# Unmasked retention products, sample states read in fours, mixer-output loads placed earlier, and gate steps moved into two stages of a hybrid decoder layer

## The chip, the cores and the metric

The kernel runs on one core of a Trainium2 chip. The metric is the device time of one execution in microseconds (us). TensorE (PE) multiplies, with its weight loads listed apart as PEld; VectorE (DVE), ScalarE (ACT) and GpSimd (POOL) work on tiles in the on-chip memory; SyncE (SP) issues most DMAs, in order, and POOL issues the gathers of cache pages. A "row" of PE is one record of the profile. A product of two plain fp32 tiles leaves two PE rows; one of fp32r tiles, and a transpose, leaves one.

## The reference, cut to what matters

One layer for 1024 prompt tokens and 64 sample tokens (8 sequences of 8 tokens), model width 1024: feed-forward, mixer, feed-forward. The mixer projects the normed input `u` once (`w_in`) and has two branches, each behind gates:

```python
# stick-breaking attention: 8 heads x 64, strictly causal; the sample tokens also see 2048 cached positions
# retention: 4 heads, key width 128, value width 256, over chunks
inner = einsum('bhcd,bhsd->bhcs', qi, ki) * decay_in      # zero where s > c
o = einsum('bhcs,bhsv->bhcv', inner, vi) + einsum('bhcd,bhdv->bhcv', qi, S) * decay_q
S = S * decay_c + einsum('bhsd,bhsv->bhdv', ki * decay_k, vi)
...
m = sigmoid(a_sb) * (o_sb @ w_sb_out) + sigmoid(a_r) * (o_r @ w_ret_out);  h = h + RMSNorm_post(m @ w_o)
```

Each sample sequence brings its own retention state of 128 x 256 per head, which is read by its 8 queries and returned updated. `decay_in` is zero above the diagonal.

## The kernel before, in words

All activations lie transposed (features on the 128 partitions, tokens along the free dimension). A product of full precision is `mm3` (L132 to L138): both factors are split into a high and a low fp32r part, and three fp32r matmuls (high weights times high data, L133; high weights times low data, L137; low weights times high data, L138) add up in one bank of PSUM. There are eight banks: two named `pa`, two `pb`, three `pc`, one `pm`.

The order of the run: the first feed-forward (0 to about 790 us), `mixer_in` (to about 1925 us), `mixer_out` (to about 2065 us), the second feed-forward, and the last norm.

`mixer_in` runs these parts:

- Retention, heads r = 0 to 3 (`retention`, L1305). A head projects queries, keys and values (`dense`), computes two gates, prepares the sample tokens, and goes over four chunks of 256 prompt tokens. A chunk transposes its keys (L1437), forms scores for two key halves s = 0, 1 against all 256 queries (`pz`), multiplies by the decay mask `rdec` (512 columns, zero above the diagonal), splits the result, multiplies it by the values (`po`), adds the state's part, normalises (`finish`) and updates the state. For s = 1 the first 128 queries lie wholly above the diagonal.
- After each chunk `sample_states` (L1388) takes two of the eight sample sequences. It loads their states into `s0` (two buffers), multiplies each with that sequence's queries, laid out as 64 columns of which 8 are not zero (L1394, fp32, 64-column weights), forms the outer products of keys and values (L1399, fp32, 128-column weights), and stores the new states from the same tile.
- The prompt's attention, heads 0 to 7 (`prompt_sb`, L889), with each pair's projections, and then the sample tokens' attention over the cache (`decode_sb`). Its pages come by 128 gathers of 512 KB (`kp`, `vp`), and its small products run four side by side, each on 32 columns of the array (`side_by_side`, L1129).

Beside these runs a list of independent tiles of work, the gates and the projection by `w_ret_out` (`gate_steps`, `ret_steps`). One step is one `mm3`; eight steps make one bank's result, which goes through a tile `gs` (three buffers) to DRAM. `fill(k)` takes k steps from the list. Before the change 40 steps are taken after the last retention head (`FILL_RET`, behind the head's last transposes), 2 at each of the 16 places of prompt heads 0, 2, 4, 6 and 7, 12 after the prompt (`FILL_SB`), and the rest in the decode at 1.6, 1.75 or 2 steps a place, until the list is empty.

The order within each engine's queue is made ahead of time by a planner, which takes the instructions by program order as their inputs come free by its own costs and keeps the hand-written ordering edges (`behind`, `high_priority`). A queue on the chip then runs strictly in that order.

`mixer_out` multiplies the attention output (`attn_parts` loads and splits it; the sample part comes from `osD`) by `w_sb_out` in three token pieces c = 0, 1, 2 of 512, 288 and 288 tokens, eight output tiles d each. Each result is multiplied by a gate tile `g` and added to a tile `m` (both `xr`, eight buffers, L1581 and L1583), and split (`mh`, `ml`). The loads of piece c + 1 are issued at d = 4 of piece c, with their split behind them.

Of the kernel before, what the change touches and what calls it, by code (L numbers as in the profile page):

```python
# [19 lines left out]
P = 128  # L20
# [21 lines left out]
FILL_RET, FILL_SB = 40, 12  # L42
# [26 lines left out]
class Trunk:  # L69
# [700 lines left out]
    def gates_out(self, specs, pool=None, ahead=()):  # L770
# [19 lines left out]

    def gate_steps(self, specs, after=None, chunks=(0, 1, 2)):
# [4 lines left out]
        for c in chunks:  # L796
            o, n = CH[c]
            for (wh, wl), (_, row, _) in zip(ws, specs):
                ps = self.bank("pa")
                for k in range(KD):  # L800
                    self.mm3(ps[:, :n], wh[:, k, :], wl[:, k, :], self.u[0][c][:, k, :n], self.u[1][c][:, k, :n],
                             k == 0, k == KD - 1)
                    if k == KD - 1:
                        g = self.t(self.gstage, [P, 384], "gs", bufs=3)
                        nc.scalar.activation(g[:, :n], ps[:, :n], AF.Sigmoid)
                        nc.sync.dma_start(row[:, o : o + n], g[:, :n])
# [52 lines left out]
    def ret_steps(self, d):  # L859
# [4 lines left out]
        for c, (o, n) in enumerate(CH):  # L864
# [3 lines left out]
            for k in range(KD):  # L868
                self.mm3(ps[:, :n], wh[:, k, :], wl[:, k, :], self.ro[0][c][:, k, :n], self.ro[1][c][:, k, :n],
                         k == 0, k == KD - 1)  # L870
                if k == KD - 1:
                    g = self.t(self.gstage, [P, 384], "gs", bufs=3)
# [5 lines left out]
    def through(self, gen, k, other=None):  # L878

        due = 0.0  # L880
        for _ in gen:
            due += k
# [6 lines left out]
    def prompt_sb(self):  # L889
        nc, io = self.nc, self.io  # L890
        win = io["w_in"][0]
        with ExitStack() as ctx:
# [95 lines left out]
            def head(h):  # L988
# [4 lines left out]
                for c in range(4):  # L993
# [29 lines left out]
                    for half in range(2):  # L1023
# [3 lines left out]
                        for g in range(i // 4, -1, -1):  # L1027
                            a = 512 * g
                            w = min(512, n - a)
                            wide = max(w, 256)  # L1030
                            ps = self.bank("pb")
                            lq = qs[:, i * P : (i + 1) * P]
                            nc.tensor.matmul(ps[:, :wide], lq, kh[:, a : a + wide], start=True, stop=False)
                            nc.tensor.matmul(ps[:, :wide], lq, kl[:, a : a + wide], start=False, stop=True)
# [28 lines left out]
            for p in range(4):  # L1063
                self.through(head(2 * p), FILL_HEADS[p][0])
                other = proj(p + 1) if p < 3 else None
                self.through(head(2 * p + 1), FILL_HEADS[p][1], other)
# [5 lines left out]
    def decode_sb(self):  # L1072
# [5 lines left out]
        with ExitStack() as ctx:  # L1078
# [169 lines left out]
            def last_block():  # L1248
# [9 lines left out]
                self.attn_parts(sh, sl, 0, 512)  # L1258
# [46 lines left out]
    def retention(self):  # L1305
        nc, io = self.nc, self.io
        win = io["w_in"][0]
        gam = [1.0 - 2.0 ** (-5 - h) for h in range(RH)]
        with ExitStack() as ctx:
# [7 lines left out]
            ddk = self.t(rp, [64, RH, NB], "ddk")  # L1317
            nc.sync.dma_start(ddk, io["c_ddk"])
            for r in range(RH):
                rdec = self.t(rp, [P, 512], "rdec")  # L1320
# [3 lines left out]
                rq = self.t(rp, [P, RC + TD], "rq")  # L1324
# [5 lines left out]
                vdn = self.t(rp, [P, 256], "vdn")  # L1330
                nc.gpsimd.memset(vdn[64:128, :], 0.0)

                def finish(src, o, n):

                    oc = self.t(rp, [P, 2, RC], "oc", bufs=2)
                    nc.scalar.activation(oc[:, :, :n], src, AF.Copy)
# [24 lines left out]
                def ev_v(vt):  # L1361
                    def ev(c, o, n, ps):
# [12 lines left out]
                        if m < n:  # L1375
                            nc.scalar.activation(vdn[:64, vt * P : (vt + 1) * P], pt[:64, 256:384], AF.Copy)
# [11 lines left out]
                def sample_states(b0):  # L1388
                    s0 = self.t(rp, [P, 2, 256], "s0", bufs=2)
                    nc.sync.dma_start(s0, io["state_ret"][0, b0 : b0 + 2, r].rearrange("b d v -> d b v"))  # L1390
                    pS = self.bank("pm")
                    for j in range(2):
                        b = b0 + j
                        nc.tensor.matmul(po_s[:64, :256], qm[:, b * 64 : (b + 1) * 64], s0[:, j, :],  # L1394
                                         start=False, stop=b == NB - 1)
# [3 lines left out]
                        nc.tensor.matmul(pS[:, j * 256 : (j + 1) * 256], km, vdn, start=True, stop=True)  # L1399
# [6 lines left out]
                sd = self.t(rp, [64, 64], "sd")  # L1406
                nc.vector.tensor_tensor(sd, pz[:64, :64], ddec, op=ALU.mult)
                qm = self.t(rp, [P, 576], "qm")
                nc.gpsimd.memset(qm, 0.0)
                nc.vector.tensor_tensor(qm.rearrange("q (b x) -> q b x", x=72)[:, :, 0:8],  # L1410
                                        qf[:, TP:T].rearrange("q (b t) -> q b t", t=8),
                                        rq[:, RC : RC + TD].rearrange("q (b t) -> q b t", t=8), op=ALU.mult)
                pt = self.bank("pc")
                nc.tensor.transpose(pt[:64, :P], kf[:, TP:T], self.ident)
                kts = self.t(rp, [64, 256], "odn")[:, :P]
                nc.scalar.activation(kts, pt[:64, :P], AF.Copy)
                po_s = self.bank("pc")
                nc.tensor.matmul(po_s[:64, :256], sd, vdn[:64, :], start=True, stop=False)
# [4 lines left out]
                for m in range(TP // RC):  # L1423
# [12 lines left out]
                    for s in range(2):  # L1436
                        nc.tensor.transpose(pt[:, s * P : (s + 1) * P],  # L1437
                                            kf[:, m * RC + s * P : m * RC + (s + 1) * P], self.ident)
# [8 lines left out]
                    sc = self.t(rp, [P, 512], "rsc")  # L1447
                    nc.vector.tensor_tensor(sc, pz, rdec, op=ALU.mult)
                    sch = self.t(rp, [P, 512], "rsch", F32R)
                    scl = self.t(rp, [P, 512], "rscl", F32R)  # L1450
# [10 lines left out]
                    for vt in range(2):  # L1461
                        vc = slice(vt * P, (vt + 1) * P)
                        out = po[:, vt * RC : (vt + 1) * RC]
                        for s in range(2):
                            a = 2 * m + s
                            cc = slice(s * RC, (s + 1) * RC)
                            self.mm3(out, vh[:, a, vc], vl[:, a, vc], sch[:, cc], scl[:, cc],
# [21 lines left out]
                    sample_states(2 * m)  # L1489

                on = self.t(rp, [64, 256], "odn")
                nc.scalar.activation(on, po_s[:64, :256], AF.Copy)
                pt = self.bank("pc")
                for vt in range(2):
                    self.last = nc.tensor.transpose(pt[:, vt * 64 : (vt + 1) * 64], on[:, vt * P : (vt + 1) * P],
                                                    self.ident[:64, :64]).ins
                finish(pt[:, :128].rearrange("q (v c) -> q v c", v=2), TP, TD)
# [39 lines left out]
    def attn_parts(self, sh, sl, o, n):  # L1537

        lf = sl.bitcast(F32)
        m = min(n, TP - o)  # L1540
        for q in range(0, 4, 2):
            qq = slice(q * P, (q + 2) * P)
            self.nc.sync.dma_start(lf[:, q : q + 2, :m], self.osT[qq, o : o + m].rearrange("(k p) t -> p k t", p=P))
            if m < n:
                self.nc.sync.dma_start(lf[:, q : q + 2, m:], self.osD[qq, :].rearrange("(k p) t -> p k t", p=P))
        for q in range(4):
# [3 lines left out]
    def mixer_out(self):  # L1550
        nc, io = self.nc, self.io
        mch = [(0, 512), (512, 288), (800, 288)]
        with ExitStack() as ctx:
# [7 lines left out]
            with ExitStack() as ctx2:  # L1561
# [240 lines left out]
def _constants():  # L1802
# [26 lines left out]
    out["c_rdec"] = rdec.reshape(P, RH, 2 * RC).astype(f)  # L1829
# [3 lines left out]
    out["c_rq"] = np.concatenate([np.exp(lg[:, None] * (c + 1.0)), np.exp(lg[:, None] * (t + 1.0))], 1).astype(f)  # L1833
# [4 lines left out]
    out["c_ddk"] = (np.exp(lg[None, :, None] * (7.0 - t)[:, None, None])  # L1838
                    * (b[:, None] == np.arange(NB)[None, :])[:, None, :] * sc).astype(f)
# [34 lines left out]
```

## Time and profile before

| | |
|---|---|
| times of three runs | 2867.34, 2871.73 (median), 2874.34 us |
| the profiled execution | 2862.49 us; span 2860.0 us, granted clock 0.99 |
| busy: PE, PEld | 2779.8 us (97%), 2638.2 us (92%) |
| busy: DVE, ACT, POOL | 2012.3 us (70%), 1244.4 us (44%), 737.5 us (26%) |
| DMA | 380.63 MB, mean 133 GB/s |

The granted clock is the share of full speed that TensorE was given. Matmuls are pipelined: a matmul's own duration in the profile (some 280 ns for 256 columns) is longer than the time to the next one's start (some 120 ns), so what a matmul costs a busy PE is read from the distance of starts, and "busy" of a group counts overlapped time once per group. A line of the table by stretches gives the stretch and its length, then the busy us (and instructions) of PE, PEld, DVE, ACT and POOL, the granted clock, the DMA engines' share and GB/s. A line of the timeline gives start and duration in us, engine, line, operation, out<-in, the shape and the count; where a merged line holds several shapes, it shows that of the first. In a grouped line stand the count, the group's busy us, the mean ns of one, and the idle time of the engine before them with what ended it.

### The profile page before, as it was taken

The page shows a single profiled execution, that of the slowest core. Times are in us where ns is not written, and L with a number is a line of the kernel's source. Part 1 is how long each engine was busy: PE and PEld are TensorE (multiplying, and loading weights), DVE is VectorE, ACT ScalarE, POOL GpSimd, SP SyncE. Part 2 cuts the span into 40 slices and gives each one's busy share as a digit, 9 for nine tenths or more (in the row PEclk, how much of TensorE's full clock was granted, in tenths as well). Part 3 has the DMA queues.
Part 4 walks back from the last instruction along what each step waited for, and adds up shares of the span by engine and source line. Part 5 has one row for each costly group of instructions (what it writes and reads, how often), then busy time and mean ns, then how long its engine had stood idle before and what let it go on. Part 6 is the DMA issues. An engine that isn't in the chain of part 4 may idle for free.

```text
span 2860.0 us, 51596 instructions
## 1 busy us (share of the span) xinstructions
PE 2779.8 (97%) x20064; PEld 2638.2 (92%) x20064; DVE 2012.3 (70%) x3918; ACT 1244.4 (44%) x2550; POOL 737.5 (26%) x677
## 2 busy tenths in 40 slices
PE   8999999999999999999999999999999999999998
PEld 7898899999989999989999888878989988999997
DVE  7888878888753644544889844445488898688776
ACT  6544444434343333334666642323354444544433
POOL 0234513333150000000001136530113434233331
PEclk9999999999999999999999999999999999999999
DMA  6434444333252323333223379986234346333421
GB/s 186 146 122 146 141 155 125 105 113 111 69 159 88 109 74 92 100 95 102 74 67 88 116 246 334 335 302 190 89 102 132 118 124 197 108 106 102 129 88 38
DMA packets 420868, 380.63 MB, mean 133 GB/s; under 512 B 30800, under 2 KB 381392, under 8 KB 420624
## 3 DMA queue, kind: packets, MB, share of 16 engines
q1 hardware_dynamic: 398352, 306.03, 34.8%
q0 software_dynamic: 22272, 71.31, 7.4%
q8 instruction: 157, 2.57, 0.4%
q14 instruction: 87, 0.71, 0.1%
HBM read 310.03 MB, written 63.05 MB: 130 GB/s over the span
## 4 chain that ended last, share of the span: by engine, by line
PE 61%; DVE 4%; DMA 2%; issue 1%; POOL 1%; ACT 0%; SPq 0%; DVEq 0%; ACTq 0%; POOLq 0%
PE pa L133 10%; PE pa L138 10%; PE pa L137 10%; PE pb L133 4%; PE pb L138 4%; PE pb L137 4%; PE pc L137 3%; PE pc L138 3%; PE pc L133 3%; PE pc L1224 2%; PE pm L1013 1%; PE pm L1129 1%; PE pb L1129 1%; PE pc L1001 1%; DVE sl L99 1%
## 5 line engine op out<-in xcount | busy, mean ns | idle before, releaser
L96 ACT ACTIVATE sh<-wr 128x512 fp32r<-128x512 f32 x592 | 339.3, 622 | 358.4 <-POOL wr L591 136.9
L133 PE MATMUL pa<-uh,wh 128*128 128x384 f32 (+1 forms) x1408 | 471.1, 335 | 4.2 <-ACT qdec L922 2.1
L138 PE MATMUL pa<-uh,wl 128*128 128x384 f32 (+1 forms) x1408 | 465.6, 331 | 0.0
L137 PE MATMUL pa<-ul,wh 128*128 128x384 f32 (+1 forms) x1408 | 464.0, 330 | 0.4 <-POOL ul L99 0.4
L99 DVE TENSOR_TENSOR sl<-wr,sh 128x512 fp32r<-128x512 f32 x592 | 398.2, 699 | 58.5 <-ACT sh L96 55.0
L133 PE MATMUL pa<-q,sh 128*128 128x256 f32 (+1 forms) x1408 | 409.2, 291 | 15.5 <-DVE p L649 7.7
L137 PE MATMUL pa<-q,sh 128*128 128x256 f32 (+1 forms) x1408 | 408.6, 290 | 2.2 <-DVE q L99 2.2
L138 PE MATMUL pa<-q,sl 128*128 128x256 f32 (+1 forms) x1408 | 407.3, 289 | 0.3 <-DVE sl L99 0.3
L137 PE MATMUL pc<-hl,whd 128*128 128x256 f32 (+2 forms) x1088 | 350.4, 324 | 2.6 <-DVE hl L99 2.6
L138 PE MATMUL pc<-hh,wld 128*128 128x256 f32 (+2 forms) x1088 | 349.9, 323 | 0.0
L133 PE MATMUL pc<-hh,whd 128*128 128x256 f32 (+2 forms) x1088 | 343.6, 324 | 4.5 <-DVE y L719 2.5
L719 DVE TENSOR_TENSOR y<-y,pc 128x256 f32<-128x256 f32 (+2 forms) x496 | 249.7, 515 | 134.5 <-PE pc L138 133.0
L133 PE MATMUL pb<-q,sh 128*128 128x288 f32 (+1 forms) x1088 | 314.7, 290 | 6.4 <-ACT sh L96 4.8
L138 PE MATMUL pb<-q,sl 128*128 128x288 f32 (+1 forms) x1088 | 314.4, 289 | 0.5 <-DVE sl L99 0.4
L137 PE MATMUL pb<-q,sh 128*128 128x288 f32 (+1 forms) x1088 | 314.7, 289 | 0.0
L133 PEld LDWEIGHTS pa<-q,sh 128*128 128x128 f32 x1408 | 266.9, 190 | 20.7 <-DVE p L649 8.7
L133 PEld LDWEIGHTS pa<-uh,wh 128*128 128x128 f32 x1408 | 266.5, 189 | 12.3 <-ACT qdec L922 3.2
L137 PEld LDWEIGHTS pa<-q,sh 128*128 128x128 f32 x1408 | 266.7, 189 | 4.9 <-DVE q L99 2.9
L137 PEld LDWEIGHTS pa<-ul,wh 128*128 128x128 f32 x1408 | 266.1, 189 | 2.0 <-POOL ul L99 0.7
L138 PEld LDWEIGHTS pa<-uh,wl 128*128 128x128 f32 x1408 | 265.8, 189 | 2.1 <-issue 1.2
L138 PEld LDWEIGHTS pa<-q,sl 128*128 128x128 f32 x1408 | 265.9, 189 | 1.5 <-DVE sl L99 0.6
L589 POOL TENSOR_TENSOR wr<-wr 128x512 f32<-128x512 f32 x76 | 108.5, 1428 | 497.4 <-DVE sl L99 493.5
(372 smaller groups left out, 5944.6 us busy)
## 6 DMA issues: line engine op xcount, KB each, us to landing
wr<-in_w_ffn_gu_dram SPq DMA_DIRECT2D x176, 512.0 KB
wrd<-in_w_ffn_down_dram SPq DMA_DIRECT2D x88, 512.0 KB
wr<-in_w_in_dram SPq DMA_DIRECT2D x56, 512.0 KB
q<-cB SPq DMA_DIRECT2D x16, 576.0 KB
wr<-in_w_o_dram SPq DMA_DIRECT2D x10, 512.0 KB
cB<-y SPq DMA_DIRECT2D x32, 144.0 KB
cB<-xr SPq DMA_DIRECT2D x32, 144.0 KB
s<-in_state_ret_dram SPq DMA_DIRECT2D x16, 256.0 KB
```

Of the source, the lines that this page charges most:

```text
L96: return self.nc.scalar.activation(dst, src, AF.Copy)
L99: (eng or self.nc.vector).tensor_tensor(dst, src, hi.bitcast(F32), op=ALU.subtract)
L133: ins = mm(ps, wh, xh, start=first, stop=False)
L137: mm(ps, wh, xl, start=False, stop=False)
L138: mm(ps, wl, xh, start=False, stop=last)
L589: tt(v1, v0, v1, op=ALU.add)
L719: nc.vector.tensor_tensor(y[p][:, d, c], y[p][:, d, c], ps[:, :n], op=ALU.add)
L1001: nc.tensor.transpose(tp[:, j * P : (j + 1) * P], bt[:, j * P : (j + 1) * P], self.ident)
L1013: ins = nc.tensor.matmul(po[:, lo:256], vs[:, j, :], ats[j // 4][x][:, j % 4, lo:256], start=(j == 0 and x == 0), stop=(j == last and x == 1))
L1129: return nc.tensor.matmul(out[32 * m : 32 * m + 32], w(m), x(m), start=first, stop=last, skip_group_check=True)
L1224: ins = nc.tensor.transpose(tp[:, i * P : (i + 1) * P], kp[i // 2][:, (i % 2) * 512 + m * P : (i % 2) * 512 + (m + 1) * P], self.ident)
```

## The change

- Unmasked products: scores and values for s = 1 take the last 128 queries only (`seen`); the mask and the split scores have 384 columns. In the prompt attention's scores, blocks of 128 keys are no longer widened to 256 columns.
- Sample states in fours: the queries of a sequence lie in 32 columns (`qs`), and `read_states` multiplies four states side by side, each on 32 columns, at chunks 0 and 2. New states come from fp32r products of `km` and `vxt`, made by a new function `under`, which stacks three high or low copies of a token's values (or keys) under each other by two transposes. `s0` has three buffers, and the first two loads go out before the chunks. The head's own sample scores and the last transposes are laid out accordingly (two products of 128 columns, four transposes).
- Steps of gates: `FILL_RET` goes from 40 to 16; in the last retention head each chunk takes 6 steps behind its own transposes; the last prompt head takes 6 steps instead of 2 at each of its last five places. Tile `gs` has two buffers.
- Mixer output: the loads of piece 1 are issued at d = 0 of piece 0, those of piece 2 at d = 6 of piece 0; the splits stay at d = 4.

```diff
-FILL_RET, FILL_SB = 40, 12
+FILL_CHUNK = 6
+FILL_RET, FILL_SB = 16, 12
+FILL_LAST = 20
...
-                g = self.t(self.gstage, [P, 384], "gs", bufs=3)
+                g = self.t(self.gstage, [P, 384], "gs", bufs=2)
...
-        for _ in gen:
-            due += k
+        for i, _ in enumerate(gen):
+            due += k if more is None else more.get(i, k)
...
-                            wide = max(w, 256)
-                            nc.tensor.matmul(ps[:, :wide], lq, kh[:, a : a + wide], start=True, stop=False)
+                            nc.tensor.matmul(ps[:, :w], lq, kh[:, a : a + w], start=True, stop=False)
...
+                self.through(head(2 * p + 1), FILL_HEADS[p][1], other,
+                             {i: 2 + FILL_LAST / 5 for i in range(11, 16)} if other is None else None)
...
+        seen = slice(0, RC), slice(RC, RC + P)
...
+                def under(src, parts, dst):
+                    xv = ux.rearrange("p (b x) -> p b x", x=32)
+                    sv = src.rearrange("p (b t) -> p b t", t=8)
+                    for i, part in enumerate(parts):
+                        if part == "h":
+                            self.hi(xv[:, :, 8 * i : 8 * i + 8], sv)
+                        else:
+                            self.lo(xv[:, :, 8 * i : 8 * i + 8], sv, xv[:, :, 0:8])
+                    pt = self.bank("pc")
+                    for g in range(2):
+                        nc.tensor.transpose(pt[:, g * P : (g + 1) * P], ux.bitcast(F32)[:, g * P : (g + 1) * P],
+                                            self.ident)
+                    self.hi(dst, pt[:, :256].rearrange("p (g x) -> p g x", x=P))
...
-                        nc.tensor.matmul(po_s[:64, :256], qm[:, b * 64 : (b + 1) * 64], s0[:, j, :],
-                                         start=False, stop=b == NB - 1)
-                        km = self.t(rp, [P, P], "km", bufs=2)
-                        nc.gpsimd.memset(km[64:128, :], 0.0)
-                        nc.vector.tensor_scalar(km[:64, :], kts, ddk[:, r, b : b + 1], None, op0=ALU.mult)
-                        nc.tensor.matmul(pS[:, j * 256 : (j + 1) * 256], km, vdn, start=True, stop=True)
...
+                def read_states(g, s0):
+                    ins = None
+                    for i in (3, 2, 1, 0):
+                        with self.tc.high_priority() if i < 3 else ExitStack():
+                            before, ins = ins, nc.tensor.matmul(
+                                po_s[32 * i : 32 * i + 32, g * 256 : (g + 1) * 256],
+                                qs[:, 32 * (4 * g + i) : 32 * (4 * g + i) + 32], s0[i // 2][:, i % 2, :],
+                                start=False, stop=g == 1, skip_group_check=True)
...
+                def new_states(b0, s0):
+                        km = self.t(rp, [P, P], "km", F32R, bufs=2)
+                        nc.scalar.activation(km, kxt[:, g, :], AF.Copy, scale=one[:, i : i + 1])
+                        nc.tensor.matmul(pS[:, j * 256 : (j + 1) * 256], km, vxt[:, g, :], start=True, stop=True)
...
-                        self.mm3(pz[:, s * RC : (s + 1) * RC], kh[:, ks], kl[:, ks], qh, ql, True, True)
+                        self.mm3(pz[:, seen[s]], kh[:, ks], kl[:, ks], qh[:, s * P :], ql[:, s * P :], True, True)
...
+                            self.mm3(out[:, s * P :], vh[:, a, vc], vl[:, a, vc], sch[:, seen[s]], scl[:, seen[s]],
                                      s == 0, m == 0 and s == 1)
...
-                    sample_states(2 * m)
+                    if m % 2 == 0:
+                        read_states(m // 2, states)
+                    new_states(2 * m, states.pop(0))
+                    if m < 2:
+                        states.append(load_states(2 * m + 4))
+                    if r == RH - 1:
+                        self.fill(FILL_CHUNK, begun)
...
-                        if d == 4 and c < 2:
-                            on = mch[c + 1]
-                            sh[c + 1], sl[c + 1] = (self.t(op, [P, 4, on[1]], f"s{x}{c + 1}", F32R) for x in "hl")
-                            self.attn_parts(sh[c + 1], sl[c + 1], *on)
+                        if c == 0 and d in (0, 6):
+                            i = 1 if d == 0 else 2
+                            sh[i], sl[i] = (self.t(op, [P, 4, mch[i][1]], f"s{x}{i}", F32R) for x in "hl")
+                            self.attn_load(sl[i], *mch[i])
+                        if c < 2 and d == 4:
+                            self.attn_parts(sh[c + 1], sl[c + 1])
```

More of the change, by code (lines that the diff above doesn't have):

```diff
@@ L1405, in retention @@
                 nc.tensor.matmul(pz[:64, :64], kf[:, TP:T], qf[:, TP:T], start=True, stop=True)
[L1406 to L1410, printed above, removed]
+                sd = self.t(rp, [P, 256], "sq", bufs=2)[:64]
+                nc.gpsimd.memset(sd, 0.0)
+                nc.vector.tensor_tensor(sd.rearrange("q (b x) -> q b x", x=32)[:, :, 0:8],
+                                        pz[:64, :64].rearrange("q (b t) -> q b t", t=8),
+                                        ddec.rearrange("q (b t) -> q b t", t=8), op=ALU.mult)
+                nc.vector.tensor_tensor(qs.rearrange("q (b x) -> q b x", x=32)[:, :, 0:8],
                                         qf[:, TP:T].rearrange("q (b t) -> q b t", t=8),
                                         rq[:, RC : RC + TD].rearrange("q (b t) -> q b t", t=8), op=ALU.mult)
[L1413 to L1416, printed above, removed]
+                ks = self.t(rp, [P, TD], "ks")
+                nc.vector.tensor_tensor(ks, kf[:, TP:T], rq[:, RC + TD :], op=ALU.mult)
+                kxt = self.t(rp, [P, 2, P], "kxt")
+                under(ks, "hlh", kxt)
                 po_s = self.bank("pc")
-                nc.tensor.matmul(po_s[:64, :256], sd, vdn[:64, :], start=True, stop=False)
+                for g in range(2):
+                    nc.tensor.matmul(po_s[:, g * 256 : (g + 1) * 256], sd[:, g * P : (g + 1) * P], vdn,
+                                     start=g == 0, stop=False, skip_group_check=True)
+                states = [load_states(0), load_states(2)]
                 st = sh = sl = None
```

86 lines of the change are left out of this document (50 added, 36 removed).

## The prediction

> **What bounds it now.** I read the page first, then the busy time by stretches, then PE's groups and its timeline around the operations that the change touches, and last the chain of waits at the three places where PE stands.
>
> ```profile
> span 2860.0 us, 51596 instructions
> ...
> PE 2779.8 (97%) x20064; PEld 2638.2 (92%) x20064; DVE 2012.3 (70%) x3918; ACT 1244.4 (44%) x2550; POOL 737.5 (26%) x677
> ```
>
> TensorE carries the time, with its weight loads close behind. The stretches say where that holds:
>
> ```profile
> 940.00:1040.00 100.00, 100.00 (x633) 94.74 (x632) 50.38 (x120) 35.73 (x80) 6.16 (x15) 1.00 0.31 91
> ...
> 1240.00:1275.00 35.00, 32.53 (x217) 28.54 (x215) 24.24 (x64) 14.29 (x35) 3.74 (x9) 1.00 0.34 107
> 1275.00:1285.00 10.00, 10.00 (x53) 9.68 (x53) 3.33 (x10) 1.17 (x4) 1.24 (x2) 0.83 0.34 109
> 1628.00:1644.00 16.00, 10.04 (x56) 7.66 (x55) 13.93 (x27) 8.62 (x18) 2.99 (x3) 0.80 0.35 119
> ...
> 1904.00:1935.00 31.00, 30.24 (x266) 21.09 (x265) 13.19 (x22) 6.72 (x10) 5.54 (x5) 1.00 0.86 298
> 1935.00:1941.00 6.00, 0.51 (x3) 0.19 (x2) 5.89 (x11) 2.47 (x6) 0.00 (x0) 0.74 0.96 306
> ```
>
> While a retention head runs beside the next head's projections (940 to 1040, one head), PE has no free time, and DVE, ACT and POOL have half or more of theirs. A PE microsecond removed there is a microsecond gained. The last head (to 1275) has nothing beside it: PE stops, and behind it the clock falls to 0.83. The last prompt head (1628 to 1644) leaves PE 6 us idle, and `mixer_out` nearly 6 us at 1935 to 1941.
>
> **Sample states: removed.** These groups go, all four heads together:
>
> ```profile
> L1394 PE MATMUL pc<-s,qm 128*64 128x256 f32 x64 | 18.1, 395 | 1.3 <-DMA s<-in_state_ret_dram 1.3
> L1399 PE MATMUL pm<-vdn,km 128*128 128x256 f32 x64 | 16.5, 380 | 0.0
> L1418 PE MATMUL pc<-vdn,sd 64*64 64x256 f32 x8 | 2.6, 402 | 0.0
> L1495 PE MATMUL pc<-ident,odn 64*128 64x64 f32 x8 | 1.3, 247 | 0.0
> L1414 PE MATMUL pc<-ident,kf 128*64 128x128 f32 x4 | 1.1, 271 | 0.0
> ```
>
> Their count shows that a plain fp32 product has two rows (32 products, 64 rows). What they take from their neighbours is read from starts:
>
> ```profile
> 944.15 0.28 PE L137 MATMUL pb<-rqhl,rkh 128*128 128x256 f32 x1
> 944.27 0.28 PE L138 MATMUL pb<-rqh,rkhl 128*128 128x256 f32 x1
> 944.48 1.08 PE L1394 MATMUL pc<-s,qm 128*64 128x256 f32 x4
> 945.49 0.44 PE L133 MATMUL pa<-uh,wh 128*128 128x384 f32 x1
> 945.76 0.34 PE L137 MATMUL pa<-ul,wh 128*128 128x384 f32 x1
> ...
> 951.57 1.03 PE L1399 MATMUL pm<-vdn,km 128*128 128x256 f32 x4
> 952.25 0.47 PE L133 MATMUL pb<-rqdh,rsh 128*128 128x256 f32 x1
> 952.55 0.28 PE L137 MATMUL pb<-rqdl,rsh 128*128 128x256 f32 x1
> ```
>
> An fp32r matmul of 256 columns starts its successor after 0.12 us (944.15 to 944.27). A pair of L1394 takes 1.01, the row before it 0.21 instead of 0.12, the row behind it 0.27, where 384 columns take 0.175 (below): 1.01 + 0.09 + 0.09 = 1.19. A pair of L1399 takes 0.68, and the row behind it 0.30 instead of 0.12: 0.86. There are 16 pairs of each: 19.0 + 13.8. With the three small groups' busy time (5.0) that is 37.8 us; the groups' own busy time, 39.6, agrees.
>
> **Sample states: added.** Nearest rows for four products side by side, and for transposes:
>
> ```profile
> 1672.49 1.07 PE L1129 MATMUL pb<-kt,qd 128*32 128x512 f32 x8
> 1673.48 0.66 PE L1224 MATMUL pc<-ident,kp 128*128 128x128 f32 x4
> ...
> 1359.17 0.33 PE L133 MATMUL pa<-uh,wh 128*128 128x384 f32 x1
> ...
> 1359.52 0.60 PE L1001 MATMUL pc<-ident,bt 128*128 128x128 f32 x4
> 1359.87 0.42 PE L138 MATMUL pa<-uh,wl 128*128 128x384 f32 x1
> ```
>
> - Reads: four fp32 products of 512 columns take 0.99 us side by side. Half the columns: from 0.50 (all of it goes with the columns) to 0.99 (none does), plus the 0.18 of L1394's neighbours. I take 0.76, near the lower end, because L1394 itself takes what its columns say. Eight groups: 6.1 (5.4 to 9.4).
> - New states: 32 fp32r products of 256 columns at 0.12: 3.8. The next row is fp32r too, so nothing is added.
> - `under`: 12 pairs of transposes. Four take 0.35, a switch costs 0.09: 0.175 + 0.09 = 0.26 a pair, 3.1.
> - Own scores `sd`: two products a head, as a pair of L1399: 4 x 0.86 = 3.4.
> - Last transposes: four a head, 4 x (0.35 + 0.09) = 1.8.
>
> Together 18.2. The sample part saves 37.8 - 18.2 = **19.6 us** of PE (16 to 20). ACT gets some 17 short operations more a head and loses none that matter; of the 100 us of a head 64 are free on ACT and 50 on DVE. Without that cover they would cost some 0.3 us each. The last head's quarter of this counts only if something fills PE there (below).
>
> **Unmasked products.** Nine matmuls a chunk, 144 in all, go from 256 to 128 columns, and 32 of the prompt's scores. The trace has such narrow ones, two at a time:
>
> ```profile
> 1348.61 0.45 PE L1013 MATMUL pm<-at,vs 128*128 128x256 f32 x3
> 1348.90 0.36 PE L137 MATMUL pa<-ul,wh 128*128 128x320 f32 x1
> 1349.10 0.30 PE L138 MATMUL pa<-uh,wl 128*128 128x320 f32 x1
> 1349.24 0.31 PE L133 MATMUL pa<-uh,wh 128*128 128x320 f32 x1
> ```
>
> The three are one of 256 columns and two of 128. They take 0.29 instead of 0.36, but the next takes 0.20 instead of 0.14. Of 0.07 gained 0.06 are given back, some 0.01 a matmul: 176 x 0.01 = **1.8 us**. Without the giving back it would be 0.035 each, 6 us; a narrow one is never slower than a wide one here, so the lower bound is 0.
>
> The Trainium skill ("TensorE: Matmul & The Clock Gate", LDWEIGHTS) has a rule that speaks against this edit: a weight load takes its columns over 1.2 GHz, 107 ns for 128, whatever moves behind it. By it 120 ns could only fall to 107, an estimate of 2.3 us in all; the rows agree.
>
> **The last retention head.** Its chain of waits:
>
> ```profile
> 1262.91 2.57 DMA ut_ret_state_sample_dram<-s
> 1265.54 2.74 DMA s<-in_state_ret_dram
> 1268.33 1.08 PE pc L1394 x4
> ```
>
> A load of states waits for the store from the same buffer, 5.3 us, and PE for both. The third buffer and the early loads take that out. PE's busy time lacks 2.5 us there (35 - 32.53), and as a row's own 0.28 covers more than the 0.12 to its successor, each of its stops hides more. Behind it 53 rows in 10 us, against 63 at full clock, are 1.6 us lost. Between 2.5 and 5.3 + 1.6 = 6.9 I take **5 us**. The cover is 24 steps of three matmuls of 0.175: 12.6 us, more than these 5 and the 4.9 that the head's sample part frees. The 16 steps left behind the head (8.4 us) have to cover its last normalising; the next projection's first two banks wait for none of that, so I cost their lack at 0.
>
> **The last prompt head.** 20 steps (10.5 us) go into a stretch where PE is idle for 6 us and has lost 2 more to the clock (0.80 of 10). They are missing at the other end: the list empties during the last group of the decode. There the gathers set the time:
>
> ```profile
> 1898.65 8.81 DMA vp<-in_cache_v_dram,rowix
> ```
>
> With the steps gone, PE frees page buffers sooner, but a gather takes 8.8 us under this load. Between 0 and 8 I take **4 us**.
>
> **`mixer_out`.**
>
> ```profile
> 1934.74 0.89 SPq L1543 DMA_DIRECT2D sl<-osT  x2
> ...
> 1934.93 0.40 PE L138 MATMUL pc<-kt,wl 128*128 128x512 f32 x1
> 1940.81 0.61 PE L133 MATMUL pb<-sh,wh 128*128 128x288 f32 x1 [5.49 <-ACT sh L96]
> ```
>
> Piece 1 is loaded when PE has run out of piece 0. The change moves its two DMAs past eight loads of `g` and `m` on SP, and piece 2's four past four and eight of the next piece. If they go out early, up to 5.9 us are gained; but DVE is busy for 5.89 of these 6 us with what comes before the split, so the split comes late anyway, and behind SP's head the loads of `g` wait if the new first one waits for a page's memory. Bounds -2 and 6; I take **2 us**.
>
> **Sum.** 19.6 + 1.8 + 5 + 4 + 2 = 32.4, so 32 us off the profiled execution's 2862.5: 2830.5. That execution lies 9.2 us under the median of the runs shown, 2871.7, from which I forecast **2840**. The terms' bounds give 17 to 46 us.
>
> **Rivals.**
> - The decode's end is bound by gathers alone and the wait of `mixer_out` stays: 4 and 2 us are not had. 26 us, 2845. For it: the 8.81 us and the DMA share of 0.86 while PE is busy. Chance 0.22.
> - The early loads do remove the whole wait: 4 us more, 2836, and with the end of the decode moving fully 2832. For it: piece 1's input was written long before. Against: DVE's 5.89. Chance 0.13.
> - Narrow matmuls run at their columns' rate when three and more follow each other: up to 0.06 each instead of 0.01, 9 us more, 2831. Against: the 0.20 at 1348.90. The skill's page has an isolated gap of 56 ns for 128 columns (Back-to-back issue gap), by which an estimate is 11 us. Chance 0.04.
> - Slower: `gs` with two buffers. A load into it now waits until the store two results earlier has landed, and SP holds everything behind it:
>
> ```profile
> 1844.27 0.38 SPq L875 DMA_DIRECT2D mrT<-gs  x1
> ...
> 1851.39 0.32 SPq L875 DMA_DIRECT2D mrT<-gs  x1
> ...
> 1857.13 0.32 SPq L873 DMA_DIRECT2D gs<-gbT  x1
> ```
>
>   Against: the load at 1857.13 goes out 12.9 us after the store that it would wait for. With 24 such results it cancels the gain at 1.3 us each and at 2.5 us each gives 2840 + 60 = 2900. Chance 0.04.
> - The order that the planner makes undoes it: the steps go ahead of the next chunk's work, the last head grows by part of the 12.6 us, and at the decode's end PE stands. Then two thirds to all of the gain is lost: about 2865. Chance 0.08.
>
> **Numbers.** My forecast has 0.49. Faster: 0.49 + 0.22 + 0.13 + 0.04 = 0.88; the last rival is the no-change case, 0.08; slower 0.04. A change of less than 0.3% (8.6 us) is about what these runs cannot tell from none. The range 2827 to 2856 takes in the bounds of the sum and leaves out the last two rivals.
>
> **What would show it.** The groups L1394 and L1399 gone; groups of four side by side at some 0.6 us; narrow rows 0.11 apart; no PE stop and clock 1.00 in the last retention head and the last prompt head; the first row of piece 1 in `mixer_out` with less than 5.5 us before it. It is wrong if those stretches still show idle PE, if waits for `gs` or for page gathers grow in the decode, or if the stretch from 860 to 1240 shortens by much less than 15 us.

## The result, and the profile after

The kernel after takes 2843.57 us (median of four runs, 2841.65 to 2850.29), the kernel before 2869.53 us beside it: a ratio of 0.9915, with a 95% interval of 0.9901 to 0.9929, or 24 us less (20 to 28). A second measurement, as `a0_after` below, gave 0.9931 (0.9917 to 0.9945). Every ratio here, and for the kernels of the experiments below, is against runs of the kernel before that were taken beside it. Their medians are not the same everywhere: 2869.53 us here, 2864.46 beside `e1_ret` to `e4_last`, 2864.17 beside `a0_after` to `e9_dec`, 2869.41 beside `e10_early` to `e13_more`. So times of different groups can be set against each other through their ratios only. The forecast was 2840 us. The two profiled executions are 17.9 us apart (2862.49 and 2844.61).

The first lines of the page after:

```profile
span 2842.6 us, 51609 instructions
...
PE 2763.8 (97%) x20068; PEld 2631.6 (93%) x20068; DVE 2006.3 (71%) x3902; ACT 1261.1 (44%) x2618; POOL 731.0 (26%) x643
```

PE's busy time fell by 16.0 us, the span by 17.4: the idle time fell by 1.4 us only. Where the time came from is read from marks, rows of PE that both timelines have. They are, in order: the first value transposes of head 0, those of the last head's last piece, the first 384-column product of the prompt's scores, the decode's first rows, its last value product, the first row of piece 1 (before it is at 1940.81, as the prediction shows), the first product by `w_o`. First before, then after:

```profile
896.94 0.49 PE L1369 MATMUL pc<-ident,rxs 128*128 128x128 f32 x3
...
1225.68 0.49 PE L1369 MATMUL pc<-ident,rxs 128*128 128x128 f32 x3
...
1328.13 0.42 PE L1033 MATMUL pb<-kh,qs 128*128 128x384 f32 x1
...
1641.89 0.69 PE L1107 MATMUL pc<-ident,knew 64*128 64x64 f32 x4
...
1922.48 0.64 PE L1129 MATMUL pm<-vp,at 128*32 128x128 f32 x16
...
1968.08 0.40 PE L133 MATMUL pb<-mh,who 128*128 128x512 f32 x1
```

```profile
898.71 0.49 PE L1399 MATMUL pc<-ident,rxs 128*128 128x128 f32 x3
...
1213.01 0.55 PE L1399 MATMUL pc<-ident,rxs 128*128 128x128 f32 x3
...
1313.52 0.42 PE L1034 MATMUL pb<-kh,qs 128*128 128x384 f32 x1
...
1630.17 0.46 PE L1109 MATMUL pc<-ident,knew 64*128 64x64 f32 x4
...
1905.07 0.65 PE L1131 MATMUL pm<-vp,at 128*32 128x128 f32 x16 [0.63 <-DMA vp<-in_cache_v_dram,rowix]
...
1923.72 0.61 PE L135 MATMUL pb<-sh,wh 128*128 128x288 f32 x1 [5.70 <-ACT sh L98]
...
1951.48 0.40 PE L135 MATMUL pb<-mh,who 128*128 128x512 f32 x1
```

The distances between marks, with what the prediction's terms give for the same stretches (the sample states' 19.6 us and the products' 1.8 spread over the heads; the 4 us for the last prompt head and the decode belong to the third and fourth line together):

| stretch | before | after | difference | predicted |
|---|---|---|---|---|
| heads 0 to 2 (first to second mark) | 328.7 | 314.3 | -14.4 | -15.8 |
| last head and steps behind it, to the first scores | 102.5 | 100.5 | -1.9 | -10.3 |
| prompt heads, to the decode's first rows | 313.8 | 316.7 | +2.9 | with the next |
| decode, to the end of its last value product | 281.2 | 275.6 | -5.7 | -4 |
| decode's end to the first product by `w_o` | 45.0 | 45.8 | +0.8 | -2 |

The profiled executions differ by up to 6 us ahead of the first mark, where all these kernels are the same; a distance between marks is free of that, a time is not. The differences add up to -18.4 before rounding, and 0.8 more is gained behind the last mark.

The groups that the prediction asked for, as the view of one line gives them after (ns of one: least, median, most; first and last start). The reads:

```profile
L1429 PE MATMUL pc<-s,qs x64: 379/391/403, 935.8 to 1249.3; 128*32 128x256 f32 x64
```

The new states:

```profile
L1442 PE MATMUL pm<-vxt,km x32: 276/282/387, 953.7 to 1271.3; 128*128 128x256 f32 x32
```

The groups `s,qm` and `vdn,km` of the kernel before (its L1394 and L1399) are gone; the kernel after numbers its lines anew. From the timeline after, a group of four and a run of narrow products:

```profile
1236.39 0.64 PE L1429 MATMUL pc<-s,qs 128*32 128x256 f32 x8
1236.96 0.45 PE L135 MATMUL pa<-uh,wh 128*128 128x384 f32 x1
1237.25 0.34 PE L139 MATMUL pa<-ul,wh 128*128 128x384 f32 x1
...
1241.80 0.27 PE L140 MATMUL pb<-rsch,rvl 128*128 128x128 f32 x1
1241.91 0.33 PE L135 MATMUL pb<-rsch,rvh 128*128 128x256 f32 x1
1242.08 0.27 PE L139 MATMUL pb<-rscl,rvh 128*128 128x256 f32 x1
1242.19 0.28 PE L140 MATMUL pb<-rsch,rvl 128*128 128x256 f32 x1
1242.31 0.22 PE L135 MATMUL pb<-rsch,rvh 128*128 128x128 f32 x1
1242.37 0.28 PE L139 MATMUL pb<-rscl,rvh 128*128 128x128 f32 x1
1242.48 0.27 PE L140 MATMUL pb<-rsch,rvl 128*128 128x128 f32 x1
1242.59 0.45 PE L1442 MATMUL pm<-vxt,km 128*128 128x256 f32 x2
```

Four products side by side (eight rows) take 0.57 us (1236.39 to 1236.96), near the 0.50 that goes with the columns. Three narrow products take 0.28 (1242.31 to 1242.59), and the wide one behind such a run takes 0.17 instead of 0.12 (1241.91): 0.45 for four where four wide ones take 0.48, so 0.01 each. Both are as estimated.

One added term was not. The head's own sample scores (`sd`) are two products a head, which the prediction priced as one pair of the old L1399. In the trace each stands alone:

```profile
1221.65 0.70 PE L1464 MATMUL pc<-vdn,sq 64*128 64x256 f32 x2
1222.28 0.45 PE L135 MATMUL pa<-uh,wh 128*128 128x384 f32 x1
1222.56 0.34 PE L139 MATMUL pa<-ul,wh 128*128 128x384 f32 x1
...
1226.67 0.70 PE L1464 MATMUL pc<-vdn,sq 64*128 64x256 f32 x2
```

One alone takes 0.63 us, and the row behind it 0.28 instead of 0.175, where two of L1399 in a row took 0.68 together. That is some 0.7 us a product instead of 0.43, or 5.8 us for the eight instead of 3.4. The 1.8 us more in heads 0 to 2 are about what those heads lack (14.4 of 15.8).

### The profile page after: what moved, and what is told of

Its sections match the earlier page's. It is cut to its first block, busy times and chain, and to the rows that moved or that the text cites. A ratio compares the mean times of both kernels' runs of the same rounds, so it can differ in the third digit from the quotient of the medians.

```text
span 2842.6 us, 51609 instructions
## 1 busy us (share of the span) xinstructions
PE 2763.8 (97%) x20068; PEld 2631.6 (93%) x20068; DVE 2006.3 (71%) x3902; ACT 1261.1 (44%) x2618; POOL 731.0 (26%) x643
## 4 chain that ended last, share of the span: by engine, by line
PE 83%; DVE 8%; issue 4%; POOL 2%; ACT 1%; DMA 1%; DVEq 0%; ACTq 0%; POOLq 0%; SPq 0%
PE pa L135 13%; PE pa L139 13%; PE pa L140 13%; PE pb L135 6%; PE pc L139 5%; PE pb L139 5%; PE pb L140 5%; PE pc L140 5%; PE pc L135 5%; PE pc L1226 2%; DVE sl L101 2%; PE pb L1131 1%; PE pm L1015 1%; PE pm L1131 1%; PE pc L1003 1%
```

## The experiments

**Parts alone.** Of these four kernels the first undoes parts of the change, and the others make one part alone. Of each edit the lines that matter are shown.

`e1_ret`: after, with `FILL_RET = 40`, no steps in the chunks, `FILL_LAST = 0`, and the mixer's loads as before (`gs` keeps its two buffers).

```diff
-FILL_RET, FILL_SB = 16, 12
-FILL_LAST = 20
+FILL_RET, FILL_SB = 40, 12
+FILL_LAST = 0
...
-                    if r == RH - 1:
-                        self.fill(FILL_CHUNK, begun)
...
```

> The kernel after, with the steps of gates and the loads of the mixer's output as in the kernel before: sample states in fours and unmasked products alone. Theory 1 (TensorE rows are gained one for one where TensorE is busy, and the last head, which has no cover here, gives nothing): 16 us less than before, three quarters of 21.4; the stretch of heads 0 to 2 shorter by 16, the last head not shorter. Theory 2 (the prediction's terms, every head alike, and the wait for the states' store gone as well): 21 to 26 us less. Rival (these two parts are not what shortened the kernel): under 10 us.

2859.26 us, ratio 0.9983 (0.9974 to 0.9992): 5 us less than before. Its profile (span 2850.9) has the heads 0 to 2 shorter by 14.4, as after, and the last head's stretch longer than before, seen in the line by stretches:

```profile
1213.10:1319.19 106.09, 98.75 (x620) 92.73 (x619) 43.78 (x106) 37.22 (x90) 10.10 (x17) 0.97 0.33 96
```

106.1 us against 102.5 before: without steps the new form of the head loses 3.6 us although it gives PE less to do. That is worse than theory 1 had it. The profiled execution was the shortest of the 11 (2852.85); where the ordinary one spends 6 us more, no profile shows, so the time alone would speak for the rival. The stretches do not.

This kernel also shows what the two buffers of `gs` cost, since its decode has the steps of before. In the decode SP waits 111.7 us in all for stores from `gs` to `mrT`, against 60.0 before; yet the decode takes 281.4 us against 281.2. So the waits cost nothing here. They do not come from the buffers alone: `e4_last`, with three, has 94.0.

`e2_prod`: before, with `seen`, the 384-column tiles and the unwidened prompt scores.

```diff
...
-                        self.mm3(pz[:, s * RC : (s + 1) * RC], kh[:, ks], kl[:, ks], qh, ql, True, True)
...
+                        self.mm3(pz[:, seen[s]], kh[:, ks], kl[:, ks], qh[:, s * P :], ql[:, s * P :], True, True)
...
```

> The kernel before, with the unmasked products alone. Theory 1 (a narrow matmul gives back what it gains, 0.01 us each): 2 us less, at most 6, rows of 128 columns some 0.11 us apart on average. Rival (their columns' rate, 0.06 us each): 9 to 11 us less, rows of 128 columns 0.06 apart in threes.

2862.50 us, 0.9991 (0.9982 to 1.0): 2.6 us less, 0 to 5. Theory 1; a gain of 9 is excluded. By the marks, the stretches up to the decode are 1.4 us shorter than before.

`e3_chunk`: before, with 24 steps inside the last retention head.

```diff
-FILL_RET, FILL_SB = 40, 12
+FILL_CHUNK = 6
+FILL_RET, FILL_SB = 16, 12
...
+                    if r == RH - 1:
+                        self.fill(FILL_CHUNK, begun)
```

> The kernel before, with 24 of the 40 steps moved into the last retention head alone. The sample states are as before here, with the load that waits for the store. Theory 1 (the head's chain sets its length, and the planner puts the steps where the chain then starts later): 0 us, between 2 less and 2 more, with PE still idle or slow by some 6 us in the head. Theory 2 (the prediction: steps fill the stops): 4 to 6 us less and no idle PE in the head.

2859.02 us, 0.9982 (0.9973 to 0.999): 5 us less. Theory 2. The last head's line in the table of stretches, before:

```profile
1225.68:1328.13 102.45, 99.98 (x621) 94.43 (x619) 45.40 (x112) 34.18 (x78) 11.40 (x23) 0.98 0.35 103
```

And in this kernel:

```profile
1227.30:1324.69 97.39, 97.39 (x620) 92.31 (x619) 46.16 (x112) 33.98 (x78) 11.67 (x23) 1.00 0.37 108
```

PE is busy throughout, the clock is 1.00, and the stretch is 5.1 us shorter. The steps do fill the old head's stops. (The decode of this profile is 1.9 us longer than before; the times do not show it.) The kernel after, with the same steps and less to compute, needs 100.5:

```profile
1213.01:1313.52 100.51, 96.73 (x620) 91.75 (x619) 44.10 (x106) 36.92 (x90) 9.78 (x17) 0.98 0.35 102
```

`e4_last`: before, with the 20 steps in the last prompt head.

```diff
+FILL_LAST = 20
...
-                self.through(head(2 * p + 1), FILL_HEADS[p][1], other)
+                self.through(head(2 * p + 1), FILL_HEADS[p][1], other,
+                             {i: 2 + FILL_LAST / 5 for i in range(11, 16)} if other is None else None)
```

> The kernel before, with 20 steps in the last prompt head alone. Theory 1 (8 us gained in the head, 5 lost at the decode's end where gathers set the time): 3 us less; the first row of the decode's key pages 2 to 3 us later than before and its last value product 3 us earlier, with 4 to 6 us of idle PE in the decode's last 40 us. Rival A (gathers set all of the decode): 0 us, the last value product where it was. Rival B (no price at the other end): 8 us less.

2862.61 us, 0.9987 (0.9977 to 0.9996): 3.7 us less. Theory 1. From the first mark to the decode's first rows it is 2.7 us longer than before for 10.5 us of steps, so 7.8 are gained; the decode is only 6.9 us shorter than before although it has 10.5 us less to do, and PE is idle for 7.3 of its last 40 us:

```profile
1647.78 0.46 PE L1109 MATMUL pc<-ident,knew 64*128 64x64 f32 x4
...
1921.03 1.08 PE L1131 MATMUL pm<-vp,at 128*32 128x128 f32 x16 [1.47 <-DMA vp<-in_cache_v_dram,rowix]
```

**What is missing in the last head.** The timeline after, at the head's end: a DMA issued on SP, then ACT, then PE.

```profile
1270.67 0.40 SPq L1377 DMA_DIRECT2D orT<-oc  x1
...
1273.03 0.60 ACT L1545 ACTIVATE oc<-pc 128x512 f32<-128x512 f32 x1 [2.80 <-DMA orT<-oc]
...
1273.68 1.11 PE L1548 MATMUL pc<-ident,oc 128*128 128x128 f32 x4 [0.47 <-ACT oc L1545]
```

The change lets `on`, the copy of the samples' output, take one of the two `oc` buffers, where before it had its own tile (`odn`). So it waits until a chunk's normalised result has been stored, the last transposes wait for it, and the 16 steps behind the head are tied to these transposes. `a0_after` is the kernel after again, as a measure; `e7_on` gives `on` a buffer of the states' ring:

```diff
-                on = self.t(rp, [P, 2, RC], "oc", bufs=2).rearrange("q v c -> q (v c)")
+                on = self.t(rp, [P, 2, 256], "s0", bufs=3).rearrange("q v c -> q (v c)")
```

> The kernel after, unchanged, as the measure of the three beside it. By both theories 20 to 28 us less than before.

2844.08 us, 0.9931 (0.9917 to 0.9945): 20 us less than before. The distances between marks repeat those above within 0.3 us, but for the decode (1.3 us shorter) and what follows it (1.0 longer).

> The kernel after, with the samples' retention output copied into a buffer of the states' ring instead of one of the two oc buffers. Theory 1 (in the last head this copy waits 2.3 to 3.4 us for the store of the normalised chunk, and the 16 steps behind the head wait for the transposes that follow it): 2 to 3 us less than after, last transposes of the head 2 us earlier. Rival (another link of the chain, VectorE's state or normalising, is as late): the time of after, within 1 us.

2841.59 us, 0.9925 (0.9913 to 0.9938), which is 2.5 us less than `a0_after`, as theory 1 had it; but the intervals cannot tell the two apart. The stretch can:

```profile
1214.60:1309.91 95.31, 93.66 (x617) 89.64 (x616) 43.04 (x105) 37.08 (x90) 10.98 (x17) 1.00 0.37 108
```

It is 5.2 us shorter than after, PE's stops down from 3.8 to 1.7 us, the clock at 1.00. Kernels whose head is that of after have 99.0 to 100.6 us here, so some 4 to 5 us of it stand. The copy now stands at 1258.70 on ACT, 16 us earlier counted from the second mark. The stretch gained more than theory 1's 3 us. The stops are 2.1 of it and the clock (0.98 to 1.00) about 2; of the 3.4 us that PE is seen to wait there in the kernel after, only 0.5 are for the copy itself. The planner also ordered the head anew, and how the gain divides between the wait and that order is not shown. Against `a0_after`, 1.5 us of it are given back in the decode and 1.7 behind the last mark; other profiles differ there by as much.

**The decode's end.** `e9_dec` is after, with

```diff
-FILL_DEC = (1.6, 1.75, 2)
+FILL_DEC = (1.45, 1.57, 2)
```

> The kernel after, with 1.45 and 1.57 steps a place in the decode instead of 1.6 and 1.75, so that the 216 steps last to the end of the last group. Theory 1 (gathers set the decode's length, wherever the steps lie): the time of after within 2 us, the idle of PE moved from the last 40 us to the groups before. Theory 2 (only the empty list at the end costs): 3 to 5 us less than after.

2835.00 us, 0.9903 (0.9888 to 0.9917): 9 us less than `a0_after`. Theory 2, and more of it than expected. The decode by stretches, after:

```profile
1626.00:1866.00 240.00, 239.16 (x2362) 204.14 (x2363) 113.22 (x202) 83.54 (x156) 120.95 (x112) 1.00 0.91 314
1866.00:1906.00 40.00, 33.45 (x410) 24.50 (x411) 12.08 (x20) 7.43 (x13) 14.10 (x15) 0.87 0.77 271
```

And in this kernel:

```profile
1622.00:1862.00 240.00, 237.51 (x2393) 202.01 (x2394) 117.54 (x206) 86.51 (x160) 123.34 (x113) 1.00 0.90 317
1862.00:1892.00 30.00, 29.46 (x365) 22.86 (x363) 8.73 (x15) 5.11 (x8) 11.75 (x13) 1.00 0.89 320
```

After, PE is full for 240 us and then idle for 6.5 of 40, at a clock of 0.87, while the DMA share falls to 0.77: PE lacks work, and the gathers are not at their limit. With the same 216 steps spread thinner the last products with the key pages come sooner (240.8 us behind the decode's first rows, where the kernel after has 245.2), the last 30 us are full, and the decode takes 266.7 us (its last value rows end at 1892.7) instead of 275.6, or 274.3 in `a0_after`.

`e12_bdec` spreads the 236 steps of the kernel before:

```diff
-FILL_DEC = (1.6, 1.75, 2)
+FILL_DEC = (1.53, 1.67, 2)
```

> The kernel before, with 1.53 and 1.67 steps a place in the decode instead of 1.6 and 1.75, so that its 236 steps last to the end. Theory 1 (in the kernel after it was the 20 steps that were missing at the end that cost 5 to 9 us; before, the list ended only 9 places early): 0 to 3 us less than before. Theory 2 (the spread itself shortens the decode, whatever is moved): 6 to 9 us less than before.

2864.68 us, 0.9987 (0.9978 to 0.9996): 3.7 us less. The decode itself did not get shorter in the profile:

```profile
1646.22 0.69 PE L1107 MATMUL pc<-ident,knew 64*128 64x64 f32 x4
...
1927.17 0.65 PE L1129 MATMUL pm<-vp,at 128*32 128x128 f32 x16
```

281.6 us, 281.2 before. That speaks for theory 1: the spread pays where steps are missing. But the profiled execution was the longest of its 11 (2869.53), and 3.7 us lie between the two theories, so it is not settled; what the 3.7 us are stays open.

**The wait ahead of piece 1.** `e6_odec` takes what waits for the last value product off VectorE:

```diff
-                        nc.vector.tensor_copy(ost[ln, :, o : o + 8], src[:, :, b2 * 16 + e * 8 : b2 * 16 + e * 8 + 8])
+                        put = nc.vector.tensor_copy if g < 3 else lambda d, x: nc.scalar.activation(d, x, AF.Copy)
+                        put(ost[ln, :, o : o + 8], src[:, :, b2 * 16 + e * 8 : b2 * 16 + e * 8 + 8])
...
-                return self.unit(src, pool=wp, sfx="o") if d in (4, 5) else self.unit(src)
+                return self.unit(src, pool=wp, sfx="o", eng=nc.gpsimd) if d in (4, 5) else self.unit(src)
```

> The kernel after, with the last group's four copies into odec on ScalarE instead of VectorE, and the two splits of the output weights (wlo) on GpSimd: VectorE then has nothing ahead of the mixer's products that waits for the last value product. Theory 1 (the wait of nearly 6 us ahead of piece 1 is VectorE working off, behind those copies, what it could have done during the 16 us in which it stood): 3 to 5 us less than after, the first row of piece 1 with under 3 us before it. Rival (the loads of piece 1, which SP issues late, set the wait): the time of after, the wait still over 5 us.

2846.44 us, 0.994 (0.9925 to 0.9954); the wait is still 5.9 us. Theory 1 as put fails, but the edit also added a cost of its own, so this run does not decide. GpSimd's timeline in it:

```profile
1907.05 5.21 POOL L101 TENSOR_TENSOR wlo<-wr,who 128x1024 fp32r<-128x1024 f32 x2 [10.50 <-PE pc L1283]
```

VectorE's timeline in the same time:

```profile
1909.92 2.89 DVE L1645 TENSOR_TENSOR xr<-xr,xr 128x512 f32<-128x512 f32 x1
1912.73 0.67 DVE L1644 TENSOR_TENSOR xr<-xr,pc 128x512 f32<-128x512 f32 x1
```

While GpSimd splits, VectorE needs 2.89 us for an addition of 0.69. And SP issues the loads of piece 1 only at 1920.18, and after at 1917.61, behind the store of `osD`, although the change had moved them forward in the source:

```profile
1912.73 0.37 SPq L1306 DMA_DIRECT2D osD<-odec  x1
...
1917.61 1.40 SPq L1596 DMA_DIRECT2D sl<-osT  x3
```

The tiles of pieces 1 and 2 share a pool that also covers the decode's last buffers. `e10_early` is after, with two pools, and with piece 1's split moved forward as well:

```diff
-                op = self.pool("mo", ctx2)
+                op = {i: self.pool(f"mo{i}", ctx2) for i in (1, 2)}
...
-                        if c < 2 and d == 4:
+                        if (c, d) in ((0, 1), (1, 4)):
```

> The kernel after, with the tiles of piece 1 and of piece 2 of the mixer's attention in two pools instead of one, and piece 1 split at the second product instead of the fifth. Piece 1 then lies only where key pages lay, and its loads and split are placed ahead of the last value product's copies. Theory 1 (the pool that both pieces share, which also covers the last buffers of the decode, held the loads back; reordering them alone could do nothing): the first row of piece 1 with under 1 us before it, 2 to 5 us less than after, less than the 5.9 because VectorE then owes the banks. Rival (VectorE's arrears set the end of the mixer's output anyway): the time of after, the wait only moved to the rows of piece 1.

2843.23 us, 0.9912 (0.9896 to 0.9927), which the intervals cannot tell from after (0.9915 and 0.9931). Its timeline, of PE and of SP (`SPq`):

```profile
1632.77 0.46 PE L1109 MATMUL pc<-ident,knew 64*128 64x64 f32 x4
...
1876.05 0.88 SPq L1596 DMA_DIRECT2D sl<-osT  x2
...
1911.27 0.64 PE L1131 MATMUL pm<-vp,at 128*32 128x128 f32 x16 [0.88 <-DMA vp<-in_cache_v_dram,rowix]
...
1921.03 0.39 PE L140 MATMUL pa<-kt,wl 128*128 128x512 f32 x1
1921.26 0.30 PE L135 MATMUL pb<-sh,wh 128*128 128x288 f32 x1
...
1949.46 0.40 PE L135 MATMUL pb<-mh,who 128*128 128x512 f32 x1
```

The loads go out 35 us ahead of the last value product, the wait is gone, and from that product to `w_o` it takes 37.6 us instead of 45.8. But the decode takes 279.1 instead of 275.6, and past this mark some 2 us more are given back. The split of piece 1 now stands inside the decode; whether it is what lengthens it is not shown. Theory 1 holds for the place; the time fits the rival as well. The two edits were not run apart.

**Together.** `e11_best` has the edits of `e7_on`, `e9_dec` and `e10_early`; `e13_more` has `FILL_CHUNK = 8` and `FILL_RET = 8` on top.

> The kernel after with three edits together: the decode's steps spread to its end (9 us less alone), the output's own buffer in the retention head (0 to 3 us less alone), the two pools of the run above. If they add up: 11 to 16 us less than after, 31 to 36 less than before. If they share one limit: 9 less than after.

2829.35 us, 0.9863 (0.9847 to 0.9879): 39 us less than before, faster than both kernels, and 13.9 us less than `e10_early` beside it, which lacks the other two edits. Alone, these took 2.5 and 9 us off `a0_after`, so they add up and share no limit that the times show.

> The kernel of the three edits with 8 steps a chunk instead of 6 in the last retention head and 8 behind it instead of 16. Theory 1 (the head's chain sets its length and every step inside it that meets no stop lengthens it): the time of the three edits within 2 us. Theory 2 (PE still has 4 us of stops there that more steps would fill): 2 to 4 us less.

2831.41 us, 0.9876 (0.986 to 0.9891), 2 us more than `e11_best` and no gain (theory 1): the stretch of the last head is 99.8 us, in `e11_best` 95.1. As in `e7_on`, a difference of 5 us in this stretch goes with one of some 2 in the times, which is within what they can tell; where the rest goes is open.

## Why the prediction was right or wrong

- **Sample states and products: right in mechanism**, where PE is full, with one term too small. Heads 0 to 2 gave 14.4 of 15.8 us; the group of four lies near its lower bound, and the narrow products gain 0.01 us each. The term "two products a head, as a pair of L1399" was 3.4 us and measures 5.8, since each of the two stands alone.
- **The last retention head: the step that failed.** "The cover is 24 steps ... more than these 5 and the 4.9 that the head's sample part frees": the steps do remove the old head's 5 us (`e3_chunk`), but the new form of the head makes a new wait. The prediction went through what the new form computes and not through where its results are put: `on` lost its own tile to a ring whose buffers wait for stores. Of 10.3 us 1.9 came; 5.2 of the missing 8.4 come with another buffer for `on` (`e7_on`). The other 3.2 stay open in part: 1.7 us of stops are still there, and the sample scores that were priced too low are 0.6.
- **Last prompt head: right.** Nearly all of the idle 6 us and the clock's 2 was had: 10.5 us of steps lengthened it by 2.7 in `e4_last` and by 2.9 after.
- **Decode's end: the size was near, the reason wrong.** Head and decode together gave 2.8 us after and 4.2 in `e4_last`, where 4 was taken. But "There the gathers set the time" is what `e9_dec` refutes, so the size was met partly by luck. The 20 steps were missing at the end because the rates were left as they were. With the thinner spread, head and decode together are 11.7 us shorter than before, more than the upper bound of 8; the 3.7 beyond it are not explained.
- **Mixer output: wrong by 2.8 us** (0.8 longer, where 2 shorter was forecast). The bounds held. The loads were moved in the source and not on the chip: they went out behind the store of `osD` as before, and with two pools 35 us ahead of the last value product. That the shared pool held them is the reading of `e10_early`, whose other edit was not taken apart from it.
- **The total and the rivals.** 32 us were forecast; the medians give 26 and 20, the marks 19. The base of 2871.7 was high too: four medians of the kernel before lie between 2864.2 and 2869.5. A base too high hides part of the miss, so that 2840 lies within 3.6 us of 2843.57 is in part luck. The first rival (26 us, 2845) has the time, and its wait ahead of piece 1 stayed; but its reason for the decode did not hold, and the last head's shortfall is not in it. Two buffers for `gs` cost nothing that the stretches show: SP's waits did grow, from 60.0 us in the decode to 73.8 after, which the prediction had named as a sign of being wrong; but the decode of `e1_ret`, where they are longest, is no longer for it. The last rival was close in kind: PE stands at the decode's end, as it said, though this kept back 4.8 of the 10.5 us of steps, and not two thirds of the whole gain.

## What to carry to other kernels

When work is moved out of a stage, ask what that stage will do at its end without it, and lower the rate of what is left so that it lasts. When a part is rewritten, cost not only its operations but the buffer that each result takes and who still has to release it. PE rows removed from a full stretch are worth their distance of starts, taken from rows that stand as the new ones will, alone or in a row; in a stretch with stops, measure the stretch and not the rows.

## What the runs showed of the hardware

- A tensor operation of GpSimd on on-chip memory can hold up VectorE: 2.89 us instead of 0.69 for one addition while GpSimd took 5.21 us for two splits. The addition ends at 1912.81, GpSimd's second split at 1912.26, 0.55 us earlier, a little less than the addition itself needs. The Trainium skill ("SBUF — State Buffer", section "SBUF: two separate sides") says that the two engines share a pair of ports as an exclusive lock, so that a VectorE operation with two inputs in this memory waits out a GpSimd operation that reads it and began first; these rows agree.
